# Token norms of a diffusion trunk: sums and modulated tiles formed in PSUM, mean squares from the token tiles, three filter units ahead of the first norm

## The chip, the cores and the metric

The kernel runs on one core of one Trainium2 chip. The metric is the device time of one execution in microseconds (us); each figure is the median of the runs named with it. TensorE is written PE in the profile's rows, VectorE DVE, ScalarE ACT, GpSimd POOL, SyncE SP.

## The reference

A trunk of four layers works on 256 latent tokens and 256 context tokens of 1,024 features (two "streams"). Each layer has a token mixer (layer 0 Hyena, 1 gated linear attention or GLA, 2 latent attention or MLA, 3 Hyena) and an MLP with squared ReLU. Each of these sub-layers first normalises and modulates its input:

```python
def rmsnorm(x, g):
    xf = x.astype(F32)
    y = xf * lax.rsqrt(jnp.mean(xf * xf, axis=-1, keepdims=True) + NORM_EPS)
    return (y * g.astype(F32)).astype(x.dtype)

def modulate(h, shift, scale):
    return h * (1 + scale) + shift

h_lat = modulate(rmsnorm(x_lat, norm1_g[i]), mod_l[0], mod_l[1])
x_lat = x_lat + mod_l[2] * y_lat
```

Shift, scale and gate are columns of `silu(c) @ ada_w[i] + ada_b[i]`, a vector of 6 x 1,024 per layer and stream (the "maps", in six parts of 1,024). Hyena convolves with long filters: a small network of position gives `h`, `h @ f_w4` gives the taps of two filters in both directions for each feature, which are decayed, divided by their absolute sum and transformed to spectra. After MLA only the latent stream goes on. The output is the latent stream after a last norm.

## The kernel before

**Layout.** The stream x lies transposed: eight tiles `x0` to `x7` of 128 features by 512 tokens (256 latent, 256 context). At the start eight token tiles `xr` (128 tokens by 512 features, L250) are loaded and TensorE transposes them into x (L325 to 329), VectorE copying from PSUM (L329).

**Products.** A product of fp32 values is made as three matmuls of rounded halves (L369 wh x uH, L370 wh x uL, L371 wl x uH). A slab of weights comes by DMA on SP's queue as `wraw` (5 buffers), ACT rounds it to `wh` (L359, 4 buffers), POOL subtracts to `wl` (L360, 4 buffers). On the activations' side ACT writes the high half `uH` and VectorE the low half `uL`.

**The norm of two streams** is `norm_mod` (L515), used five times: ahead of Hyena 0, its MLP, GLA, its MLP, and MLA. For each stream `token_rstd` (L481) squares eight x tiles (on ACT, L490; in the opening on POOL, L488), adds seven of them up on VectorE (L497), lets TensorE sum over features (L501) and forms 1/rms in `rsqrt` (L474 to 478: two steps on ACT, three on VectorE). `token_diag` (L510, VectorE) and one matmul (L524) spread it over a PSUM bank `rb`. Then for each of eight tiles k: VectorE multiplies x by scale and 1/rms into `t`, an SBUF tile named xr (L528), ACT adds the shift and rounds to uH (L529), VectorE makes uL (L530). The norm of one stream, `lone_norm` (L570 to 626), used in the rest, already holds its input and its running sum in PSUM (L584, L585, L592, L594); its statistics L599 to 615 use the same `rsqrt` and `token_diag` and lead to the matmul L610. The last norm of all calls `token_rstd` (L1642).

**The banks.** The eight PSUM banks are handed out by tags: mm two, cv three, ada one, st two. Buffers of one tag are handed out in the order in which the code asks for them. First products of Hyena's unit 0, of GLA and of MLA go to mm; of the MLP's first product, chunks 2 and 3 go to cv and the others to mm.

**The maps.** Each part of the maps takes eight slabs of 512 KB, multiplied as they come (L407 load, L410 matmul); `ada_part` (L388 to 394) writes the shifts and `adam`, the scales. `pump(n)` lets n slabs go into the program at the place where it is called.

**The opening.** After the filter network (L300, L309) comes the first norm, then `filters` (L896): eight units, each of `taps` (L813 to 848: load of w4r, ACT and POOL split it at L822 and L823, matmuls L832 and L833, decay, four POOL operations at L836 to L847), `scaled` (L850 to 868: column sums L854, L855, division and split) and `spectra` (L870 to 894: 24 matmuls of 256 columns, copies, a store). The units' temporaries have one buffer each. In the stretch that the profile calls unit 0 and 1, `project` makes the three parts of a 128-feature unit: unit 0 in halves of one stream each (144 matmuls of 256 columns), later ones over both streams (512 columns). Ahead of MLA the products of the latent stream (pq, 384 columns, to mm) and then the KV products (pk, 320 columns, mostly to cv) follow the norm.

**Order.** A planner places each engine's instructions in one static order; the order of the program is its priority. It chooses among what its own timeline holds ready. `tc.issue_after(x)` keeps what is in it behind x.

The norm's core, before:

```python
for k in range(KD):
    t = np_.tile([P, SEQ], F32, tag="xr", name=nm("xr"))
    sc, sh = a[:, which, k, r : r + 1], m[:, 3 * which, k, r : r + 1]
    nc.vector.scalar_tensor_tensor(t, xT[k][:, s], sc, rb[:, :SEQ], ALU.mult, ALU.mult)
    nc.scalar.activation(uH[k][:, s], t, AF.Identity, bias=sh)
    nc.vector.scalar_tensor_tensor(uL[k][:, s], t, sh, rounded(uH[k][:, s]), ALU.add, ALU.subtract)
```

Of the kernel before, what the change touches and what calls it, by code (L numbers as in the profile page):

```python
# [18 lines left out]
P = 128  # L19
# [108 lines left out]
def trunk_kernel(ctx: ExitStack, tc: tile.TileContext, ins: dict, table, zpos, out, layers=(0, 1, 2, 3)):  # L128
# [123 lines left out]

    if need_hy:
# [70 lines left out]
    xT = [cp.tile([P, TOK], F32, tag=f"x{k}", name=f"x{k}") for k in range(KD)]  # L324
    for k in range(KD):  # L325
        ps = bank("cv")
        for j in range(4):
            nc.tensor.transpose(ps[:, j * P : (j + 1) * P], xr[2 * j + k // 4][:, (k % 4) * P : (k % 4 + 1) * P], ident)
        nc.vector.tensor_copy(xT[k], ps)  # L329
# [140 lines left out]
    def rsqrt(v, n):  # L470

        y = np_.tile([P, n], F32, tag="rs_y", name=nm("rsy"))
        t = np_.tile([P, n], F32, tag="rs_t", name=nm("rst"))
        nc.scalar.activation(t, v, AF.Ln)  # L474
        nc.scalar.activation(y, t, AF.Exp, scale=-0.5)
        nc.vector.scalar_tensor_tensor(t, y, -0.5, y, ALU.mult, ALU.mult)
        nc.vector.tensor_tensor(t, t, v, ALU.mult)
        nc.vector.scalar_tensor_tensor(y, t, 1.5, y, ALU.add, ALU.mult)
        return y

    def token_rstd(r, on_pool=False):  # L481

        s = slice(r * SEQ, (r + 1) * SEQ)
        acc = np_.tile([P, SEQ], F32, tag="sacc", name=nm("sacc"), bufs=1)

        def square(dst, k):
            if on_pool:
                nc.gpsimd.tensor_tensor(dst, xT[k][:, s], xT[k][:, s], ALU.mult)  # L488
            else:
                nc.scalar.activation(dst, xT[k][:, s], AF.Square)  # L490

        square(acc, 0)
        for k in range(1, KD):
            sq = np_.tile([P, SEQ], F32, tag="sq", name=nm("sq"))
            square(sq, k)
            if k < KD - 1:
                nc.vector.tensor_tensor(acc, acc, sq, ALU.add)  # L497
        ps = bank("st")
        for j in range(2):
            for e, a in enumerate((acc, sq)):  # L500
                nc.tensor.matmul(ps[:, 2 * j : 2 * j + 2], a[:, j * P : (j + 1) * P], ones[:, 0:2],  # L501
                                 start=e == 0, stop=e == 1)
        v = np_.tile([P, 2], F32, tag="rs_v", name=nm("rsv"))
        nc.vector.tensor_scalar(v, ps[:, 0:4:2], 1.0 / D, EPS, ALU.mult, ALU.add)
        return rsqrt(v, 2)

    def token_diag(y):
        diag = np_.tile([P, 2, P], F32, tag="sq", name=nm("diag"))
        for j in range(2):
            nc.vector.tensor_scalar(diag[:, j], ident, y[:, j : j + 1], None, ALU.mult)  # L510
        return diag
# [3 lines left out]
    def norm_mod(i, which, nt, first=False):  # L515
# [3 lines left out]
        uL = [up.tile([P, TOK], F32R, tag=f"uL{k}", name=nm("uL")) for k in range(KD)]  # L519
        def stream(r):  # L520
            s = slice(r * SEQ, (r + 1) * SEQ)
            y = token_rstd(r, first)
            rb = bank("st")
            nc.tensor.matmul(rb[:, :SEQ], ones, token_diag(y), start=True, stop=True)  # L524
            for k in range(KD):
                t = np_.tile([P, SEQ], F32, tag="xr", name=nm("xr"))
                sc, sh = a[:, which, k, r : r + 1], m[:, 3 * which, k, r : r + 1]
                nc.vector.scalar_tensor_tensor(t, xT[k][:, s], sc, rb[:, :SEQ], ALU.mult, ALU.mult)  # L528
# [42 lines left out]
    def lone_norm(i, which, mp):  # L571
# [27 lines left out]
        def statistics():  # L599
            ps = bank("st")  # L600
            for j in range(2):
                for e, a in enumerate((acc, sq)):
                    nc.tensor.matmul(ps[:, 2 * j : 2 * j + 2], a[:, j * P : (j + 1) * P], ones[:, 0:2],
                                     start=e == 0, stop=e == 1)
            v = np_.tile([P, 2], F32, tag="rs_v", name=nm("rsv"))
            nc.vector.tensor_scalar(v, ps[:, 0:4:2], 1.0 / D, EPS, ALU.mult, ALU.add)
            diag = token_diag(rsqrt(v, 2))
# [72 lines left out]
    def mlp(i, nt, later=None, lone=()):  # L680
        single = nt == SEQ
        if not single:
            u = norm_mod(i, 1, nt)
# [226 lines left out]
    def hyena(i, j, nt, build):  # L910

        two = nt == TOK
        if two:
            u = norm_mod(i, 0, nt, build)
        if not build:
            pump(8, 8)
        nct = 1 if two else 2
        units = KD // nct
        with tc.tile_pool(name=nm("hy"), bufs=2, reuse_waits="tile") as mp:
# [62 lines left out]
            if build:  # L982
                with tc.tile_pool(name=nm("fs"), bufs=1) as fp:
                    tabs = dft_table(fp, "dftt", fp, "odd")
                    ftab = dft_table(mp, "dftf", fp, "odd")
                    gtab = dft_table(mp, "dftg", fp, "odd")
                    for _ in filters(j, fp, tabs, "cv", False):
# [167 lines left out]
    def gla(i, j):  # L1155
# [4 lines left out]
        u = norm_mod(i, 0, nt)  # L1160
# [213 lines left out]
    def mla(i, j):  # L1374
        nt = TOK
        QR, KVR = 384, 256
        u = norm_mod(i, 0, nt)
# [226 lines left out]

    with tc.issue_after(chain.ins) if chain is not None else ExitStack():
        pump(14 if len(layers) == DEPTH else 38)
# [35 lines left out]
    y = token_rstd(0)  # L1642
# [39 lines left out]
```

## Time and profile before

| | |
|---|---|
| median of 3 runs | 2199.26 us (2194.21 to 2200.56) |
| the profiled execution | 2200.74 us |
| its span | 2199.0 us |
| mean granted clock of TensorE | 0.97 |

The span goes from the first to the last instruction that the trace records. In a timeline a row is the start, the duration, engine, line, operation, output and inputs; behind it, in brackets, the idle time of the engine before it and what ended that. Two operations of one engine overlap a little in such rows, as it is pipelined: "x2" with 0.86 us is two operations one behind the other. The granted clock is a share of 2.4 GHz; 0.50 is the lower of two levels, 1.2 GHz.

### The profile page before, as it was taken

What the parts mean: (1) busy time and instruction counts of PE and PEld (TensorE: products, weight loads), DVE (VectorE), ACT (ScalarE), POOL (GpSimd) and SP (SyncE); (2) the same over time, 40 slices, a digit from 0 to 9 for tenths busy, and PEclk for the clock granted to TensorE, in tenths of its full rate; (3) what the DMA queues carried; (4) which work ended last, traced back from release to release, by engine and by line L of the source; (5) the groups of instructions that cost most, each with busy time, mean ns of one, the idle gap of its engine ahead of it and who ended that gap; (6) DMA issues with size and microseconds to landing.
All of it is one profiled execution on the core that took longest, in us unless ns stands there. A gap on an engine that the chain in (4) does not pass through costs nothing. (4 is left out here: it accounts for less than half of the span.)

```text
span 2199.0 us, 33332 instructions
## 1 busy us (share of the span) xinstructions
PE 2076.9 (94%) x12834; PEld 1767.8 (80%) x12834; DVE 1300.7 (59%) x2442; ACT 907.8 (41%) x1529; POOL 1088.2 (49%) x637
## 2 busy tenths in 40 slices
PE   6998999989999999999889999998999998898998
PEld 3766687677888888878678777788789998888998
DVE  7863888765333335554675987677673224895323
ACT  2642333343333334554442222235445546544544
POOL 5662454346545433333224444334346887455885
PEclk8998999989999999999999999999999999999999
DMA  9666635533333332222216788853235665443663
GB/s 313 192 213 203 222 100 178 193 99 118 103 99 107 108 92 71 81 58 67 58 49 220 220 278 266 265 185 96 65 91 169 186 189 159 144 135 108 191 182 116
DMA packets 322301, 329.12 MB, mean 150 GB/s; under 512 B 21276, under 2 KB 248673, under 8 KB 322143
## 3 DMA queue, kind: packets, MB, share of 16 engines
q1 hardware_dynamic: 321012, 326.05, 47.8%
q8 instruction: 101, 1.65, 0.3%
q10 hardware_dynamic: 587, 0.61, 0.1%
q14 instruction: 57, 0.47, 0.1%
q0 software_dynamic: 544, 0.34, 0.1%
HBM read 317.51 MB, written 9.44 MB: 149 GB/s over the span
## 5 line engine op out<-in xcount | busy, mean ns | idle before, releaser
L360 POOL TENSOR_TENSOR wl<-wraw,wh 128x1024 fp32r<-128x1024 f32 (+2 forms) x378 | 907.1, 2413 | 898.7 <-ACT wh L359 850.9
L359 ACT CAST wh<-wraw 128x1024 fp32r<-128x1024 f32 (+2 forms) x378 | 391.0, 1042 | 634.0 <-PE mm L370 238.5
L369 PE MATMUL mm<-uH,wh 128*128 128x512 f32 (+3 forms) x1272 | 449.4, 356 | 15.0 <-ACT uH L584 5.4
L370 PE MATMUL mm<-uL,wh 128*128 128x512 f32 (+3 forms) x1272 | 449.3, 354 | 8.5 <-DVE uL L530 5.8
L371 PE MATMUL mm<-uH,wl 128*128 128x512 f32 (+3 forms) x1272 | 444.7, 351 | 0.0
L369 PEld LDWEIGHTS mm<-uH,wh 128*128 128x128 f32 (+1 forms) x1272 | 245.0, 194 | 58.2 <-issue 8.7
L370 PEld LDWEIGHTS mm<-uL,wh 128*128 128x128 f32 (+1 forms) x1272 | 246.3, 194 | 44.4 <-DVE uL L530 9.6
L371 PEld LDWEIGHTS mm<-uH,wl 128*128 128x128 f32 (+1 forms) x1272 | 245.9, 193 | 32.5 <-issue 3.8
L369 PE MATMUL cv<-fH,wh 128*128 128x512 f32 (+1 forms) x576 | 209.7, 370 | 9.6 <-ACT fH L176 6.7
L370 PE MATMUL cv<-fL,wh 128*128 128x512 f32 (+1 forms) x576 | 210.7, 367 | 0.7 <-DVE fL L177 0.6
L371 PE MATMUL cv<-fH,wl 128*128 128x512 f32 (+1 forms) x576 | 208.9, 366 | 0.0
L663 DVE SCALAR_TENSOR_TENSOR x<-cv,mods,x 128x256 f32<-128x256 f32 x256 | 112.2, 477 | 83.2 <-PE cv L371 83.2
L370 PE MATMUL sum<-fL,wh 128*128 128x256 f32 x512 | 138.8, 278 | 0.0
L369 PE MATMUL sum<-fH,wh 128*128 128x256 f32 x512 | 137.2, 278 | 0.0
L371 PE MATMUL sum<-fH,wl 128*128 128x256 f32 x512 | 136.7, 278 | 0.0
L369 PEld LDWEIGHTS cv<-fH,wh 128*128 128x128 f32 x576 | 108.0, 189 | 31.9 <-ACT fH L176 8.4
L715 DVE SCALAR_TENSOR_TENSOR mm<-mm,r 128x512 f32<-128x512 f32 x60 | 41.7, 696 | 139.9 <-ACT r L714 139.7
L370 PEld LDWEIGHTS cv<-fL,wh 128*128 128x128 f32 x576 | 108.6, 189 | 19.0 <-DVE fL L177 1.1
L371 PEld LDWEIGHTS cv<-fH,wl 128*128 128x128 f32 x576 | 108.6, 189 | 17.8 <-issue 0.2
L369 PE MATMUL mm<-oH,wh 128*128 128x256 f32 (+1 forms) x256 | 92.0, 361 | 18.9 <-DVE x L663 14.2
L436 DVE SCALAR_TENSOR_TENSOR st<-lw,sT,st 128x512 f32<-128x512 f32 x144 | 101.4, 747 | 9.8 <-DMA lw<-in_ada_w_dram 9.8
L618 DVE COPY rbias<-st 128x1 f32<-128x1 f32 x32 | 5.1, 159 | 163.1 <-PE st L371 162.8
(526 smaller groups left out, 4513.8 us busy)
## 6 DMA issues: line engine op xcount, KB each, us to landing
wraw<-in_mlp_w_dram SPq DMA_DIRECT2D x256, 512.0 KB
adaw<-in_ada_w_dram SPq DMA_DIRECT2D x96, 512.0 KB
lw<-in_ada_w_dram SPq DMA_DIRECT2D x96, 512.0 KB
wraw<-in_hy_w_in_dram SPq DMA_DIRECT2D x48, 512.0 KB
wraw<-in_gla_w_in_dram SPq DMA_DIRECT2D x24, 512.0 KB
spec<-S SPq DMA_DIRECT2D x16, 512.0 KB
wraw<-in_hy_w_out_dram SPq DMA_DIRECT2D x16, 512.0 KB
S<-spec SPq DMA_DIRECT2D x32, 256.0 KB
```

The lines of the kernel that those rows point to most:

```text
L359: nc.scalar.copy(wh[r0:r1, :n], raw[r0:r1, :n])
L360: nc.gpsimd.tensor_tensor(wl[r0:r1, :n], raw[r0:r1, :n], rounded(wh[r0:r1, :n]), ALU.subtract)
L369: nc.tensor.matmul(ps, lh, rh, start=start, stop=False)
L370: nc.tensor.matmul(ps, lh, rl, start=False, stop=False)
L371: nc.tensor.matmul(ps, ll, rh, start=False, stop=stop)
L436: nc.vector.scalar_tensor_tensor(dst, wt[:, cols], sT[:, k, 0:1], run[b], ALU.mult, ALU.add)
L618: nc.vector.tensor_copy(bias, ps[:, SEQ : SEQ + 1])
L663: add = nc.vector.scalar_tensor_tensor(xT[dt][:, q], ps[:, q], mods[i][:, gi, dt, r : r + 1], xT[dt][:, q], ALU.mult, ALU.add)
L715: nc.vector.scalar_tensor_tensor(r, r, 0.0, pos, ALU.max, ALU.mult)
```

## The change

The first norm's mean squares are taken from the token tiles: ACT squares each with a sum along the features, and one `rsqrt` of four columns serves both streams. The copies of x alternate between VectorE and ACT. Three units of the filters are put into the program ahead of the first norm, with 8 and 6 slabs of the maps between them in place of the 14 that stood behind the filter network. In the norm of two streams the running sum, the steps of 1/rms and the tile t lie in PSUM: t takes half a bank, two k to a bank, of the tag given (mm, or cv ahead of the MLP). Sums, 1/rms and `rb` of a stream share one st bank. ACT instead of VectorE makes the diagonal. ACT computes the Exp of 1/rms a second time, into PSUM. The statistics of the one-stream norm and the last norm use the same new `rsqrt` and `token_diag`.

```diff
+    def transpose_in(k):
...
+        (nc.scalar.copy if k % 2 else nc.vector.tensor_copy)(xT[k], ps)
...
+    sums = cp.tile([P, 8], F32, tag="xsum", name="xsum")
+    junk = wp.tile([P, SLOT], F32, tag="wl", name="junk", bufs=4)
+    for b in range(8):
+        nc.scalar.activation(junk[:, :512], xr[b], AF.Square, accum_out=sums[:, b : b + 1])
+    means = cp.tile([P, 4], F32, tag="xmean", name="xmean")
+    nc.vector.tensor_tensor(means, sums[:, 0:8:2], sums[:, 1:8:2], ALU.add)
+    nc.vector.tensor_scalar(means, means, 1.0 / D, EPS, ALU.mult, ALU.add)
...
-    def rsqrt(v, n):
+    def rsqrt(v, n, ps=None):
...
         nc.scalar.activation(t, v, AF.Ln)
         nc.scalar.activation(y, t, AF.Exp, scale=-0.5)
-        nc.vector.scalar_tensor_tensor(t, y, -0.5, y, ALU.mult, ALU.mult)
+        y2 = y
+        if ps is not None:
+            y2 = ps[:, :n]
+            nc.scalar.activation(y2, t, AF.Exp, scale=-0.5)
+            t = ps[:, n : 2 * n]
+        nc.vector.scalar_tensor_tensor(t, y2, -0.5, y, ALU.mult, ALU.mult)
         nc.vector.tensor_tensor(t, t, v, ALU.mult)
         nc.vector.scalar_tensor_tensor(y, t, 1.5, y, ALU.add, ALU.mult)
...
-    def token_rstd(r, on_pool=False):
+    def token_rstd(r, ps):
...
+        run = ps[:, :SEQ]
         acc = np_.tile([P, SEQ], F32, tag="sacc", name=nm("sacc"), bufs=1)
...
+        for k in range(KD):
+            sq = np_.tile([P, SEQ], F32, tag="sq", name=nm("sq")) if k else None
+            nc.scalar.activation(sq if k else run, xT[k][:, s], AF.Square)
+            if 0 < k < KD - 1:
+                nc.vector.tensor_tensor(acc if k == KD - 2 else run, run, sq, ALU.add)
+        st = ps[:, SEQ : SEQ + 4]
...
+        return rsqrt(v, 2, ps[:, SEQ + 4 : SEQ + 8])
...
-            nc.vector.tensor_scalar(diag[:, j], ident, y[:, j : j + 1], None, ALU.mult)
+            nc.scalar.activation(diag[:, j], ident, AF.Copy, scale=y[:, j : j + 1])
...
-    def norm_mod(i, which, nt, first=False):
+    def norm_mod(i, which, nt, tag, known=None):
...
-            y = token_rstd(r, first)
-            rb = bank("st")
-            nc.tensor.matmul(rb[:, :SEQ], ones, token_diag(y), start=True, stop=True)
+            ps = bank("st")
+            y = token_rstd(r, ps) if known is None else known[:, 2 * r : 2 * r + 2]
+            rb = ps[:, :SEQ]
+            nc.tensor.matmul(rb, ones, token_diag(y), start=True, stop=True)
             for k in range(KD):
-                t = np_.tile([P, SEQ], F32, tag="xr", name=nm("xr"))
+                if k % 2 == 0:
+                    t2 = bank(tag)
+                t = t2[:, k % 2 * SEQ : (k % 2 + 1) * SEQ]
...
-        u = norm_mod(i, 0, nt, build)
         if not build:
+            if two:
+                u = norm_mod(i, 0, nt, "mm")
             pump(8, 8)
...
                     tabs = dft_table(fp, "dftt", fp, "odd")
+                    spectra_ = filters(j, fp, tabs, "cv", False)
+                    next(spectra_)
+                    pump(8)
+                    next(spectra_)
+                    pump(6)
+                    next(spectra_)
+                    u = norm_mod(i, 0, nt, "mm", rsqrt(means, 4))
                     ftab = dft_table(mp, "dftf", fp, "odd")
                     gtab = dft_table(mp, "dftg", fp, "odd")
-                    for _ in filters(j, fp, tabs, "cv", False):
+                    for _ in spectra_:
                         pump(1, 8)
...
     pump(2)
-
-    with tc.issue_after(chain.ins) if chain is not None else ExitStack():
-        pump(14 if len(layers) == DEPTH else 38)
```

The MLP calls `norm_mod` with tag cv, GLA and MLA with mm; `statistics` of the one-stream norm and the last norm pass their st bank to `rsqrt`.

## Rows read from the trace of the kernel before

**Rows 1.** The page's first part: busy time, share of the span, instructions per engine.

```profile
PE 2076.9 (94%) x12834; PEld 1767.8 (80%) x12834; DVE 1300.7 (59%) x2442; ACT 907.8 (41%) x1529; POOL 1088.2 (49%) x637
```

**Rows 2.** Windows, 41.0 to 85.2: length; PE, PEld, DVE, ACT, POOL busy; clock, DMA, GB/s.

```profile
41.00:85.20 44.20, 40.35 (x263) 30.77 (x264) 39.77 (x61) 24.05 (x42) 26.52 (x19) 0.81 0.83 253
```

**Rows 3.** Timeline of the opening; from 79.33 to 85.07 there are 49 matmuls.

```profile
40.49 0.47 DVE L528 SCALAR_TENSOR_TENSOR xr<-x,adam,st 128x256 f32<-128x256 f32 x1
...
55.32 0.58 PE L370 MATMUL mm<-uL,wh 128*128 128x256 f32 x1 [1.73 <-DVE uL L530]
...
79.33 0.38 PE L369 MATMUL mm<-uH,wh 128*128 128x256 f32 x1
...
85.19 0.40 PE L369 MATMUL mm<-uH,wh 128*128 128x512 f32 x1
```

**Rows 4.** Groups of PE, 41.0 to 85.2: busy us, mean ns | idle before.

```profile
L410 PE MATMUL ada<-adaw,sT 128*32 128x256 f32 x64 | 6.6, 465 | 0.0
L833 PE MATMUL cv<-w4l,h 64*128 64x512 f32 x4 | 2.3, 620 | 0.0
...
L832 PE MATMUL cv<-w4h,h 128*128 128x512 f32 x4 | 2.2, 590 | 0.0
L855 PE MATMUL cv<-ab,ones 128*1 128x256 f32 x4 | 1.2, 377 | 0.0
```

**Rows 5.** Groups of POOL, 41 to 180 us, all eight filter units.

```profile
L847 POOL TENSOR_TENSOR eo<-hd 128x512 f32<-128x512 f32 x8 | 11.8, 1476 | 0.2
L823 POOL TENSOR_TENSOR w4l<-w4r,w4h 64x512 fp32r<-64x512 f32 x8 | 11.6, 1453 | 3.8 <-ACT w4h L822 3.8
...
L842 POOL TENSOR_TENSOR ab<-ab,eo 128x512 f32<-128x512 f32 x8 | 10.3, 1285 | 1.0 <-ACT eo L841 1.0
```

**Rows 6.** Single lines, whole span: ns minimum/median/maximum, first and last start, forms.

```profile
L530 DVE SCALAR_TENSOR_TENSOR uL<-xr,mods,uH x80: 466/483/3628, 41.6 to 1524.3; 128x256 fp32r<-128x256 f32 x80
L497 DVE TENSOR_TENSOR sacc<-sacc,sq x66: 407/418/2315, 18.2 to 2190.2; 128x256 f32<-128x256 f32 x66
L585 DVE SCALAR_TENSOR_TENSOR uL<-sum,adam,uH x24: 472/476/485, 1645.3 to 1998.3; 128x256 fp32r<-128x256 f32 x24
L594 DVE TENSOR_TENSOR mm<-mm,sq x15: 417/433/433, 1648.5 to 1999.2; 128x256 f32<-128x256 f32 x15
L528 DVE SCALAR_TENSOR_TENSOR xr<-x,adam,st x80: 461/473/483, 40.5 to 1522.4; 128x256 f32<-128x256 f32 x80
```

**Rows 7.** L530 by norm: 0 to 100, 425 to 480, 820 to 880, 1480 to 1530 us.

```profile
L530 DVE SCALAR_TENSOR_TENSOR uL<-xr,mods,uH 128x256 fp32r<-128x256 f32 x16 | 13.0, 828 | 1.8 <-ACT uH L529 1.8
...
L530 DVE SCALAR_TENSOR_TENSOR uL<-xr,mods,uH 128x256 fp32r<-128x256 f32 x16 | 13.1, 839 | 0.4 <-ACT uH L529 0.4
...
L530 DVE SCALAR_TENSOR_TENSOR uL<-xr,mods,uH 128x256 fp32r<-128x256 f32 x16 | 9.4, 611 | 0.7 <-ACT uH L529 0.7
...
L530 DVE SCALAR_TENSOR_TENSOR uL<-xr,mods,uH 128x256 fp32r<-128x256 f32 x16 | 12.0, 781 | 1.4 <-ACT uH L529 1.3
```

**Rows 8.** Timeline of the norm ahead of MLA, DVE and PE.

```profile
1498.02 0.44 PE L369 MATMUL mm<-wh,uH 128*128 128x384 f32 x1
...
1509.17 2.09 DVE L478 SCALAR_TENSOR_TENSOR rsy<-rst,rsy 128x2 f32<-128x2 f32 x1
...
1516.33 0.33 PE L371 MATMUL mm<-wh,uL 128*128 128x384 f32 x1
...
1520.11 0.86 DVE L528 SCALAR_TENSOR_TENSOR xr<-x,adam,st 128x256 f32<-128x256 f32 x2
```

**Rows 9.** Windows, all engines, ahead of the first MLP's products (columns as in rows 2).

```profile
475.00:480.00 5.00, 3.28 (x8) 2.61 (x9) 5.00 (x8) 3.97 (x8) 5.00 (x2) 0.50 0.59 166
```

**Rows 10.** Timeline of the one-stream norm ahead of the last MLP.

```profile
2006.87 2.34 DVE L476 SCALAR_TENSOR_TENSOR rst<-rsy 128x2 f32<-128x2 f32 x1 [0.95 <-ACT rsy L475]
2009.63 2.57 DVE L510 TENSOR_SCALAR diag<-ident,rsy 128x128 f32<-128x128 f32 x2
...
2012.25 0.70 PE L610 MATMUL st<-diag,ones 128*128 128x256 f32 x2 [3.65 <-DVE diag L510]
```

More of the change, by code (lines that the diff above doesn't have):

```diff
@@ L251, in trunk_kernel @@
         xr.append(t)
+    def transpose_in(k):
+        ps = bank("cv")
+        for j in range(4):
+            nc.tensor.transpose(ps[:, j * P : (j + 1) * P], xr[2 * j + k // 4][:, (k % 4) * P : (k % 4 + 1) * P], ident)
+        (nc.scalar.copy if k % 2 else nc.vector.tensor_copy)(xT[k], ps)
     if need_hy:
@@ L324, in trunk_kernel @@
     xT = [cp.tile([P, TOK], F32, tag=f"x{k}", name=f"x{k}") for k in range(KD)]
+    sums = cp.tile([P, 8], F32, tag="xsum", name="xsum")
[5 more added lines that the diff above has]
+    nc.vector.tensor_scalar(means, means, 1.0 / D, EPS, ALU.mult, ALU.add)
     for k in range(KD):
[L326 to L329, printed above, removed]
+        transpose_in(k)
     pre = nc.scalar.preload_act_table_set("natural_log_exp_and_others")
@@ L479, in rsqrt @@
         return y
-    def token_rstd(r, on_pool=False):
+    def token_rstd(r, ps):
         s = slice(r * SEQ, (r + 1) * SEQ)
+        run = ps[:, :SEQ]
         acc = np_.tile([P, SEQ], F32, tag="sacc", name=nm("sacc"), bufs=1)
[L486 to L498, printed above, removed]
+        for k in range(KD):
[4 more added lines that the diff above has]
+        st = ps[:, SEQ : SEQ + 4]
         for j in range(2):
             for e, a in enumerate((acc, sq)):
-                nc.tensor.matmul(ps[:, 2 * j : 2 * j + 2], a[:, j * P : (j + 1) * P], ones[:, 0:2],
+                nc.tensor.matmul(st[:, 2 * j : 2 * j + 2], a[:, j * P : (j + 1) * P], ones[:, 0:2],
                                  start=e == 0, stop=e == 1)
         v = np_.tile([P, 2], F32, tag="rs_v", name=nm("rsv"))
-        nc.vector.tensor_scalar(v, ps[:, 0:4:2], 1.0 / D, EPS, ALU.mult, ALU.add)
-        return rsqrt(v, 2)
+        nc.vector.tensor_scalar(v, st[:, 0:4:2], 1.0 / D, EPS, ALU.mult, ALU.add)
+        return rsqrt(v, 2, ps[:, SEQ + 4 : SEQ + 8])
     def token_diag(y):
@@ L521, in stream @@
             s = slice(r * SEQ, (r + 1) * SEQ)
-            y = token_rstd(r, first)
-            rb = bank("st")
-            nc.tensor.matmul(rb[:, :SEQ], ones, token_diag(y), start=True, stop=True)
+            ps = bank("st")
+            y = token_rstd(r, ps) if known is None else known[:, 2 * r : 2 * r + 2]
+            rb = ps[:, :SEQ]
+            nc.tensor.matmul(rb, ones, token_diag(y), start=True, stop=True)
             for k in range(KD):
-                t = np_.tile([P, SEQ], F32, tag="xr", name=nm("xr"))
+                if k % 2 == 0:
+                    t2 = bank(tag)
+                t = t2[:, k % 2 * SEQ : (k % 2 + 1) * SEQ]
                 sc, sh = a[:, which, k, r : r + 1], m[:, 3 * which, k, r : r + 1]
-                nc.vector.scalar_tensor_tensor(t, xT[k][:, s], sc, rb[:, :SEQ], ALU.mult, ALU.mult)
+                nc.vector.scalar_tensor_tensor(t, xT[k][:, s], sc, rb, ALU.mult, ALU.mult)
                 nc.scalar.activation(uH[k][:, s], t, AF.Identity, bias=sh)
@@ L600, in statistics @@
             ps = bank("st")
+            st = ps[:, SEQ : SEQ + 4]
             for j in range(2):
                 for e, a in enumerate((acc, sq)):
-                    nc.tensor.matmul(ps[:, 2 * j : 2 * j + 2], a[:, j * P : (j + 1) * P], ones[:, 0:2],
+                    nc.tensor.matmul(st[:, 2 * j : 2 * j + 2], a[:, j * P : (j + 1) * P], ones[:, 0:2],
                                      start=e == 0, stop=e == 1)
             v = np_.tile([P, 2], F32, tag="rs_v", name=nm("rsv"))
-            nc.vector.tensor_scalar(v, ps[:, 0:4:2], 1.0 / D, EPS, ALU.mult, ALU.add)
-            diag = token_diag(rsqrt(v, 2))
+            nc.vector.tensor_scalar(v, st[:, 0:4:2], 1.0 / D, EPS, ALU.mult, ALU.add)
+            diag = token_diag(rsqrt(v, 2, ps[:, SEQ + 4 : SEQ + 8]))
             def rstd():
@@ L682, in mlp @@
         if not single:
-            u = norm_mod(i, 1, nt)
+            u = norm_mod(i, 1, nt, "cv")
         with ExitStack() as es:
@@ L912, in hyena @@
         two = nt == TOK
-        if two:
-            u = norm_mod(i, 0, nt, build)
         if not build:
+            if two:
+                u = norm_mod(i, 0, nt, "mm")
             pump(8, 8)
@@ L1159, in gla @@
         w_in = g["gla_w_in"][j]
-        u = norm_mod(i, 0, nt)
+        u = norm_mod(i, 0, nt, "mm")
         pump(8, 8)
@@ L1376, in mla @@
         QR, KVR = 384, 256
-        u = norm_mod(i, 0, nt)
+        u = norm_mod(i, 0, nt, "mm")
         pump(8, 8)
@@ L1641, in trunk_kernel @@
         transposed(k)
-    y = token_rstd(0)
+    y = token_rstd(0, bank("st"))
     transposed(KD - 1)
```

## The prediction

> **What bounds the kernel now.** I read the page's busy line first: TensorE is busy 2076.9 us of the 2199.0 us span [rows 1]. So about 122 us are all that can be won by better order, and an engine is worth speeding up only where TensorE stands still behind it. Next I cut the span by windows of TensorE. The first large loss is the stretch from the first modulated tile to the first product of Hyena's second unit, 41.0 to 85.2 us, where TensorE is busy for 40.35 us of 44.20 but at a granted clock of 0.81, and VectorE for 39.77 [rows 2]. The timeline of that stretch shows its frame: the first modulated tile begins at 40.49, the first 512-column product of unit 1 at 85.19, and in between TensorE waits for a low half on VectorE [rows 3]. The groups of TensorE [rows 4] say what it had to do there, those of POOL what a filter unit costs that engine [rows 5].
>
> Then I asked why VectorE is slow in the norms. The low half L530 takes 483 ns at its median and 3628 at its worst, the sum L497 418 and 2315; the same kinds of operation with one operand in PSUM never leave their price: L585 472 to 485, L594 417 to 433, and L528, which stands between the L530s in the same norms, 461 to 483 [rows 6]. An SBUF-only operation of VectorE is sometimes held for the length of a POOL subtraction; one that reads or writes PSUM is not. By norm, sixteen L530 should cost 16 x 0.483 = 7.7 us and cost 13.0 in the opening, 13.1 ahead of the first MLP, 9.4 ahead of GLA (ahead of the second MLP the same to 0.1) and 12.0 ahead of MLA: 5.3, 5.4, 1.7, 1.7 and 4.3 us are held time [rows 7]. 0.3% of this kernel, 6.6 us, is about what a measurement can tell from no change.
>
> **The opening.** Removed: POOL's 16 squares, 12 sums, four little products, both 1/rms chains. Added: 8 ACT squares, two small VectorE operations, one rsqrt of four columns; they need only the token tiles, there long before 40.49, when the first scales arrive, and the wait for these covers them, so I cost them at nothing; uncovered, eight squares of 512 columns would be between 8 x 0.42, the sum of 256 columns on VectorE [rows 6], and twice that: 3 to 7 us. Half of the x copies go to ACT, at nothing for the same reason.
>
> Moved: three filter units come ahead of the norm. Work that TensorE does in 41.0 to 85.2: unit 0's 144 products at (85.19 - 79.33)/49 = 0.12 us [rows 3] are 17.2; the ada slabs 6.6; two taps 2.2 + 2.3; two scale steps 1.2 for L855 and about as much for their column sums [rows 4]; one unit of spectra, 24 products x 0.12 = 2.9. Sum 33.6 of 44.2, so 10.6 are lost. Three units cost POOL 3 x (1.45 + 1.29 + 2 x 1.48) = 17.1 us [rows 5]; TensorE's part, 3 x (2.9 + 2.25 + 1.2) = 19.1 us, fits into what is now bare: the slabs' arrival and the norm. The norm starts later: the DFT table and one unit's taps and decay, 0.8 MB, stand ahead of slabs on SP's queue, 3 us at 253 GB/s [rows 2], up to 6 if all three units' do. Its 32 VectorE operations at about 0.43 (two L528 in 0.86 [rows 8]) take 13.9 us, with filter work between, so unit 0 starts at about 60 instead of the first products at 42; but from there it runs dense, and what stood behind it is done. I take 8 of the 10.6 back, the rest goes to the clock's second rise and gaps. Bounds: +14 (all of it and 3 idle us before 41) and -3 (the slabs 6 us late, 3 of it uncovered): **+8**.
>
> **Sums, 1/rms and t in PSUM; ACT makes the diagonal.** Per norm the held time can go. Ahead of the first MLP, VectorE and POOL are both busy all of 475 to 480 us while TensorE has 3.28 of 5 at half clock [rows 9]; of 5.4 I count 3, since the first products (four chunks per stream) end earlier but the two streams then leave a gap: **+3** (0 to +5.4). Ahead of GLA 1.7 held: **+1** (-3 to +5); ahead of the second MLP **0** (-5 to +2). In the single-stream norms two small operations were held, 2.34 us and 2.57 for two, with TensorE 3.65 us idle behind the last [rows 10]; the PSUM operand and ACT's diagonal take those away: **+4** (0 to +4.6). The final norm gains an Exp of two columns on the path of the end: **-0.3**.
>
> Here a rule speaks against the change. The rows have an L530-like operation with its source in PSUM at 476 ns against 483 from SBUF, a sum at 433 against 418 [rows 6]: the operand's place costs -7 to +15 ns. The Trainium skill, "VectorE: DVE Perf Modes", section on the TRN2 errata, lists 58 + FD cycles for SBUF to SBUF and 120 + FD for PSUM to SBUF, at 0.96 GHz, some 65 ns more for a PSUM source. By it 32 operations per norm cost 2 us more, and three such norms on the path take 6 off the sum. I go by the rows.
>
> **The banks.** This is the added wait. t takes a PSUM bank per two k, eight pairs per norm, out of two "mm" banks (three "cv" ahead of the MLP). The first products of Hyena, GLA and MLA also write "mm", and banks of a tag go round in turn, so none of them can begin before stream 1's sixth tile has left its bank. Behind the waiting product on TensorE stand the others of its chain; and the weight slabs that it holds keep the next ones out. In Hyena this costs nothing as long as filter work is there, which is why I start unit 0 at 60. Ahead of MLA there is no such work: now the 48 products of the latent stream begin at 1498.02, with stream 0's first halves, and end at 1516.33 [rows 8], while VectorE is still at stream 1. Stream 1's fifth and sixth tile are formed at 1520.11 and on. Of that, some 9 us are held time that goes: 4.3 in L530, 1.9 in one step of the 1/rms [rows 7, 8], and about 2.8 in the sums, an estimate within their worst single one, 2.3 against 0.4 [rows 6]. So the bank comes free near 1513, after the two L530 of that pair. The 48 products, of 384 columns each and so 1.5 x 0.12 = 0.18 us apart, are 8.6 us, and two more at half clock: an end at 1523.5, **-7** (0, where the KV products with "cv" banks go first; -10, where they wait for slabs too).
>
> **Sum.** 8 + 3 + 1 + 0 + 4 - 0.3 - 7 = 8.7 us gained against the profiled execution's own 2200.74, which stands 1.5 above the median of 2199.26: 2192.0, and 2190.5 against the median. I say **2190**.
>
> **Rivals.**
> 1. *The bank decides* (slower). For it: every first product of GLA, MLA and the MLPs' third and fourth chunk waits for a bank behind 32 VectorE operations, where now it starts on the first halves, and in such a stretch the granted clock was 0.50 [rows 9]. Against: before, the same products ran at DVE's pace anyway. Price: MLA 10, GLA 3, second MLP 5, the opening at its old pace and 3 late, less 4 from the single-stream norms and 3 at the first MLP: 14, so 2213. It decides once TensorE's idle time from a residual's end to the sixth tile exceeds the held time taken away (5.4 and 4.3 at the most).
> 2. *The opening does not do what it says*: TensorE has no slack later, and what is done early is only moved; the filters' pace is POOL's and ACT's. Then 0 in the opening, MLA -5, the rest as above: 2196.5.
> 3. *Opening recovered whole*, +14, MLA -3: 2180.
> 4. *PSUM operands are dear.* If each of VectorE's 32 operations per norm took 22 ns more, the spread of L528 in rows 6, on the path of three norms, 2 us would be lost: 2192.5. The medians of rows 6 speak against it. The Trainium skill's page on VectorE named above would have it at 6 us, 2196.5.
>
> **How the numbers follow.** Forecast 0.45, rival 1 0.19, rival 2 0.22, rival 3 0.12, rival 4 0.02. Faster by over 6.6 us is under 2192.7: 0.33 of the forecast, all of rival 3, 0.07 of rivals 2 and 4: 0.52. Within: 0.12 of the forecast, 0.16 of rivals 2 and 4: 0.28. Slower, over 2205.9: rival 1 and a remainder of rival 2, 0.20. The range goes from 2175, the opening at its bound with MLA unharmed, to 2210, two thirds of the way into rival 1. Both signs do not hold most of the chance alike: the forecast's own range is 2183 to 2198.
>
> **What would show it.** Right: L530 and L497 without long cases; in the opening three units of spectra before the first product of unit 0, which begins near 60 and runs at 0.12 us; unit 1's first 512-column product by 77 plus the moved filter work; MLA's first product at 1512 or so of the old time scale, with TensorE idle before it and at half clock after. Wrong: TensorE's windows between 41 and 100 with as much idle as before; GLA or the second MLP with a new wait of over 3 us on a t tile; L528 or L530 at 540 ns; or the held time still there, moved to another operation on SBUF alone (the squares' and filters' own).

## The result: slower, and where the profile after says so

The changed kernel takes 2221.35 us (median of 4 runs, 2219.48 to 2226.88), the kernel before 2197.04 in the same runs: a ratio of 1.0117, 95% interval 1.0099 to 1.0134. That is 24 us slower, outside the forecast's range and on its other side. The execution profiled after took 2226.88 (span 2225.1), the slowest of its four; that of before, 2200.74, was among the slower of its own too, and that of the last column below, 2170.40, the fastest of its six (median 2179.62). So stage times from the traces are good to some microseconds, and the medians carry the sums.

I cut the traces at the start of the last residual add of each stage, of the first add in the first row, and of the eighth (the last before a gap) in the row on MLA's first residual. Differences are after less before, in us; the other columns are experiments told below (1, 2 and 6), each against the same trace of before.

| to the end of | before | changed | preload held | copies only | norms alone |
|---|---|---|---|---|---|
| opening, layer 0's first add | 262.7 | -20.5 | -8.6 | +3.7 | -5.1 |
| layer 0's mixer | 436.3 | -5.5 | +1.0 | +12.3 | -7.8 |
| first MLP | 842.5 | -10.8 | -1.1 | +12.6 | -13.9 |
| GLA | 1119.3 | +11.3 | -6.6 | +36.0 | -16.8 |
| second MLP | 1500.4 | +8.9 | -8.0 | +38.9 | -20.5 |
| MLA's first residual | 1607.0 | +28.4 | +4.1 | +45.9 | -20.8 |
| last layer's MLP | 2188.9 | +22.9 | -1.3 | +46.7 | -32.0 |

Read downward, the changed kernel loses 15 in layer 0's mixer, 22 in GLA and 19.5 up to MLA's first residual, and wins in the MLPs and in the last layers. The page's first part after, which answers to [rows 1], shows TensorE with the same work and ScalarE 99 us busier (907.8 before):

```profile
PE 2078.6 (93%) x12818; PEld 1766.6 (79%) x12818; DVE 1238.8 (56%) x2397; ACT 1006.8 (45%) x1650; POOL 1074.9 (48%) x621
```

The part of the theory about held operations is right. Single lines after (ns minimum/median/maximum), which answer to [rows 6]: the low half is now L544, the modulated tile L542, the sum L506. Each has two forms, by the bank or tile that it reads or writes.

```profile
L544 DVE SCALAR_TENSOR_TENSOR uL<-mm,mods,uH x48: 462/476/486, 42.7 to 1527.6; 128x256 fp32r<-128x256 f32 x48
L544 DVE SCALAR_TENSOR_TENSOR uL<-cv,mods,uH x32: 465/477/485, 429.4 to 1151.5; 128x256 fp32r<-128x256 f32 x32
L542 DVE SCALAR_TENSOR_TENSOR mm<-x,adam,st x48: 467/484/491, 41.1 to 1526.5; 128x256 f32<-128x256 f32 x48
L542 DVE SCALAR_TENSOR_TENSOR cv<-x,adam,st x32: 477/484/490, 427.9 to 1150.5; 128x256 f32<-128x256 f32 x32
L506 DVE TENSOR_TENSOR st<-st,sq x45: 421/432/433, 407.3 to 2214.1; 128x256 f32<-128x256 f32 x45
L506 DVE TENSOR_TENSOR sacc<-st,sq x9: 386/415/424, 417.7 to 2214.7; 128x256 f32<-128x256 f32 x9
```

No case is longer than 491 ns, where L530 had gone to 3628 and L497 to 2315. By the medians of the larger groups, PSUM operands cost -7 ns in L544, +11 in L542, +14 in L506.

One of the prediction's own signs of being wrong came true: TensorE stands idle for longer between 41 and 100 us. Its windows (length; PE, PEld, DVE, ACT, POOL busy; clock, DMA share, GB/s), before and then after, leave 3.9 and 14.1 us idle:

```profile
41.00:100.00 59.00, 55.15 (x338) 42.57 (x339) 48.64 (x70) 35.59 (x64) 39.45 (x34) 0.86 0.75 224
```

```profile
41.00:100.00 59.00, 44.92 (x301) 33.59 (x301) 45.24 (x72) 29.93 (x50) 36.08 (x26) 0.80 0.82 233
```

ScalarE's extra time was in no step of the prediction. These are its groups of table loads, before and then after (busy us, mean ns | idle before):

```profile
L180 ACT ACT_TABLE_LOAD x1 | 1.3, 1283 | 0.7 <-PEq L1667 0.7
L331 ACT ACT_TABLE_LOAD x1 | 1.3, 1283 | 0.0
```

```profile
L485 ACT ACT_TABLE_LOAD x18 | 23.1, 1283 | 0.3
L484 ACT ACT_TABLE_LOAD x18 | 23.1, 1283 | 0.3
L1175 ACT ACT_TABLE_LOAD x13 | 16.7, 1283 | 0.2
L1242 ACT ACT_TABLE_LOAD x6 | 7.7, 1283 | 0.1
L1265 ACT ACT_TABLE_LOAD x4 | 5.1, 1283 | 0.1
L1174 ACT ACT_TABLE_LOAD x4 | 5.1, 1283 | 0.1
L301 ACT ACT_TABLE_LOAD x2 | 2.6, 1283 | 0.0
L180 ACT ACT_TABLE_LOAD x1 | 1.3, 1283 | 0.7 <-PEq L1687 0.7
L341 ACT ACT_TABLE_LOAD x1 | 1.3, 1283 | 0.0
```

67 loads of 1283 ns stand where two stood. L484 and L485 are Ln and Exp of the 1/rms, the lines from 1174 on GLA's gates. ScalarE's timeline of the opening after shows how it came about:

```profile
21.83 1.28 ACT L341 ACT_TABLE_LOAD   x1
...
24.17 0.20 ACT L484 ACTIVATE rst<-xmean 128x4 f32<-128x4 f32 x1
24.39 1.28 ACT L301 ACT_TABLE_LOAD   x1
25.68 0.42 ACT L301 ACTIVATE scr<-scr 128x256 f32<-128x256 f32 x1
26.12 1.28 ACT L485 ACT_TABLE_LOAD   x1
27.41 0.21 ACT L485 ACTIVATE rsy<-rst 128x4 f32<-128x4 f32 x1
...
29.60 1.28 ACT L301 ACT_TABLE_LOAD   x1
33.88 0.63 ACT L301 ACTIVATE scr<-scr 128x512 f32<-128x512 f32 x1 [2.99 <-DVE scr L300]
```

L341 is the kernel's preload of the one table that holds both Ln and Exp. The call behind it pins it to the ScalarE instruction traced just before. In the kernel before, that was a rounding of the filter network's result, so the preload stood behind the last sine. In the changed kernel it is the copy of the last x tile, which waits for no sine: the preload goes out at 21.83, two sines come after it and fetch their own table, and from then on nearly every Ln and Exp of the 1/rms fetches one (18 of 19 each), as does each change from one to the other in GLA's gates. TensorE waits behind this chain in a head of GLA (1.24 us at 929.60, for the `sg` of L1243; four such waits in GLA, 3.4 us, where run 1 below has none):

```profile
923.94 1.28 ACT L1175 ACT_TABLE_LOAD   x1
925.24 0.63 ACT L1175 ACTIVATE sg<-sg 128x512 f32<-128x512 f32 x1
...
926.89 1.28 ACT L1242 ACT_TABLE_LOAD   x1
...
929.35 1.28 ACT L1175 ACT_TABLE_LOAD   x1
...
931.30 1.28 ACT L1265 ACT_TABLE_LOAD   x1
```

The Trainium skill, "ScalarE: Activation LUTs", section "Table sets: the hidden batching unit", counts Ln followed by Exp as one load, because one set has both. The rows differ: L484 and L485 have a load each, 18 times over. One set served both only where the preload named it.

MLA's part looks otherwise. TensorE's timeline ahead of MLA's first products after, which answers to [rows 8]:

```profile
1511.43 0.36 PE L510 MATMUL st<-ones,sq 128*128 128x2 f32 x2
...
1517.79 1.22 PE L536 MATMUL st<-diag,ones 128*128 128x256 f32 x2 [6.00 <-ACT diag L519]
1526.16 0.69 PE L379 MATMUL mm<-wh,uH 128*128 128x384 f32 x1 [7.15 <-DVE uL L544]
```

The first product begins some 17 us behind the second MLP's last add (1509.3), where before it began 2.4 us ahead of it (1498.02 against 1500.4). It waits 7.15 us for VectorE's low halves although stream 0's were ready long since: the bank. The 6.00 us ahead hold two table loads. So two theories stood: **T**, the table loads, and **B**, the wait for a PSUM bank, which was the prediction's first rival.

### The profile page after: what moved, and what is told of

The parts are those of the page before. It is cut to its first block, busy times and chain, and to the rows that moved or that the text cites. A ratio compares the mean times of both kernels' runs of the same rounds, so it can differ in the third digit from the quotient of the medians.

```text
span 2225.1 us, 33349 instructions
## 1 busy us (share of the span) xinstructions
PE 2078.6 (93%) x12818; PEld 1766.6 (79%) x12818; DVE 1238.8 (56%) x2397; ACT 1006.8 (45%) x1650; POOL 1074.9 (48%) x621
## 5 line engine op out<-in xcount | busy, mean ns | idle before, releaser
L379 PE MATMUL mm<-uH,wh 128*128 128x512 f32 (+3 forms) x1272 | 444.2, 352 | 17.6 <-ACT uH L543 6.7
L379 PE MATMUL mm<-oH,wh 128*128 128x256 f32 (+1 forms) x256 | 94.1, 369 | 22.8 <-DVE x L678 16.8
L678 DVE SCALAR_TENSOR_TENSOR x<-mm,mods,x 128x256 f32<-128x256 f32 x176 | 79.4, 477 | 30.3 <-PE mm L381 29.5
```

The source lines that it names most:

```text
L379: nc.tensor.matmul(ps, lh, rh, start=start, stop=False)
L678: add = nc.vector.scalar_tensor_tensor(xT[dt][:, q], ps[:, q], mods[i][:, gi, dt, r : r + 1], xT[dt][:, q], ALU.mult, ALU.add)
```

## Experiments

All times are medians, in us; beside them stands the ratio to runs of the kernel before on the same chip, with its 95% interval. The ratio is worked out from all runs of both kernels and can differ a little from the quotient of the two medians. Runs 1 to 4, 5 to 8, 9 and 10, 11 and 12 stand on four chips, where the kernel before has medians of 2196.66, 2195.89, 2196.02 and 2194.79. The intervals reach 3 to 4 us either way, so a difference of under some 5 us between two of these runs is not clear of noise.

**1. The preload held behind the filter network.**

```diff
-            nc.scalar.copy(dst[:fw], hv[:fw])
+            h3_copy = nc.scalar.copy(dst[:fw], hv[:fw])
...
-    pre = nc.scalar.preload_act_table_set("natural_log_exp_and_others")
+    with tc.issue_after(h3_copy.ins):
+        pre = nc.scalar.preload_act_table_set("natural_log_exp_and_others")
```

> The changed kernel with one thing altered: the preload of ScalarE's function table (ln and exp together) is held behind the filter network's last copy, as it stood before the change, so that it comes after the last sine. Theory T (table loads): in the changed kernel the preload slipped ahead of two sines, since the last ScalarE instruction traced before it is now a copy of x; the sines fetch their own table back, and from there on each Ln and each Exp fetches one of its own: 67 loads of 1.28 us where there were 2. T expects 2 loads, the 22 us lost in GLA's mixer all but gone, some 5 to 8 of the 19.5 lost ahead of and in MLA's, and 3 to 5 elsewhere: 2185 to 2197 us against 2221 for the changed kernel. Theory B (the wait for a PSUM bank ahead of GLA's and MLA's first products makes the loss; table loads lie beside it): no more than 8 us back, 2213 or above.

2203.73 us, 1.0022 (1.0010 to 1.0034): two loads, and 18 us back. That is 7 above T's range, since with the preload held everything up to the first MLP's end comes 9.7 later than in the changed kernel; but GLA's part is T's throughout: it went from +22.0 against before to -5.6. The window from the first MLP's end to GLA's (length; PE, PEld, DVE, ACT, POOL busy; clock, DMA share, GB/s), in the changed kernel and here:

```profile
831.90:1130.80 298.90, 265.42 (x1448) 218.92 (x1447) 144.42 (x267) 178.70 (x303) 86.42 (x37) 0.94 0.21 61
```

```profile
841.60:1112.80 271.20, 254.08 (x1448) 213.58 (x1447) 146.21 (x267) 128.65 (x265) 88.17 (x37) 0.98 0.23 67
```

The same 1448 matmuls, 50 us less of ScalarE, 28 us less in length. What is left of the loss sits ahead of MLA: +12 in the table above.

**2. The copies alone in the kernel before.**

```diff
-        nc.vector.tensor_copy(xT[k], ps)
+        (nc.scalar.copy if k % 2 else nc.vector.tensor_copy)(xT[k], ps)
```

> The kernel before with one line of the change: four of the eight copies of x go to ScalarE; nothing else of the change, so no PSUM bank is asked for that was not before. The preload is then free to slip ahead of the sines. T expects some 69 table loads and a loss in every norm and in GLA: 2215 to 2235 us against 2197. B expects no change within 4 us, or a gain of 1 to 2 from VectorE's four copies fewer.

2247.54 us, 1.0222 (1.0209 to 1.0236), 51 us slower, above T's range: 69 loads, 23 us lost in GLA, 12 by the end of layer 0, 7 ahead of and in MLA. B expected nothing. One line in the opening, four copies of at most 0.59 us each in the changed kernel's timeline, makes the whole loss and more, and 1 takes the loads away with the copies in place. T is shown. By stage, GLA and MLA's part pay alike in both (23 and 7 us here, 28 and 7 between 1 and the changed kernel). But up to the first MLP's end this kernel is 13 later than before, while the changed kernel is 10 earlier than 1; part of that is what ScalarE may do early there (see 7).

**3. t in SBUF ahead of GLA and MLA**, on top of 1.

```diff
-                if k % 2 == 0:
+                if tag is None:
+                    t2 = np_.tile([P, SEQ], F32, tag="xr", name=nm("xr"))
+                elif k % 2 == 0:
                     t2 = bank(tag)
...
-        u = norm_mod(i, 0, nt, "mm")
+        u = norm_mod(i, 0, nt, None)
```

> As the first of these runs (preload held), and ahead of GLA and MLA the modulated tile t lies in SBUF again, one tile per k, so that GLA's and MLA's first products wait for no bank; sums, 1/rms and the diagonal stay as changed. If the bank is a second cause beside the tables: faster than the first run by 8 to 14 us, all of it between MLA's norm and its first products, GLA within 3. If the tables are the only one: within 3 us of the first run, or slower by up to 6, as the low halves are held behind GpSimd again (4.3 and 1.7 us before the change).

2195.25 us, 0.9988 (0.9974 to 1.0001): 8.5 faster than 1. From the second MLP's end to MLA's first residual it takes what it took before (-0.2), against +12.1 in 1; GLA's first part is 3 us longer than in 1. B is a second cause, in MLA.

**4. The opening alone in the kernel before**, with the preload held as in 1 and every norm's tiles in SBUF (the change's means, copies and three filter units ahead).

```diff
+    for b in range(8):
+        nc.scalar.activation(junk[:, :512], xr[b], AF.Square, accum_out=sums[:, b : b + 1])
...
+                    spectra_ = filters(j, fp, tabs, "cv", False)
+                    next(spectra_)
...
+                    u = norm_mod(i, 0, nt, rsqrt(means, 4))
...
-        pump(14 if len(layers) == DEPTH else 38)
```

> The kernel before with the opening alone: mean squares from the token tiles, copies of x alternating, preload held behind the filter network, three filter units ahead of the first norm, the first norm's 1/rms from the known means; every norm's sums, 1/rms and t stay in SBUF as before. If the opening's gain is real and kept: the first residual add of layer 0 comes some 20 us early, about 7 of it from slabs of the maps put off, and the time is 2184 to 2191 against 2197. If what the opening wins is handed back in the layer behind it: 2194 to 2199.

2208.39 us, 1.0047 (1.0033 to 1.0062). Not 2184 to 2191, and worse than handed back. The first residual add comes 7.8 us early; the end of layer 0's mixer is 3.4 late. More on this at 11.

**5. t in SBUF ahead of MLA alone**, on top of 1: the edit of 3, with its call changed in MLA only.

```diff
     def mla(i, j):
...
-        u = norm_mod(i, 0, nt, "mm")
+        u = norm_mod(i, 0, nt, None)
```

> The first of these runs (the changed kernel with the table preload held behind the filter network), and t in SBUF ahead of MLA alone; ahead of GLA it stays in PSUM. By stage, t in SBUF in both places was 12 us shorter from the second MLP's end to MLA's first residual and 3 us longer in GLA's first part. If the bank costs in MLA only: MLA's stage back to 107 us, GLA's as in the first run, and 2190 to 2194 us in all. If the bank's wait and the held low halves just trade places in both (the sum is set by something else): 2195 to 2200, as with SBUF in both.

2188.89 us, 0.9970 (0.9954 to 0.9986): 15 faster than 1, MLA's stage (from the second MLP's end to MLA's first residual) 106.9 against 118.7. The bank's cost lies ahead of MLA; the stage shows 12 of the 15.

**6. The norms alone**: the kernel before, with PSUM sums, 1/rms, t and ScalarE's diagonal in all norms but the opening's, and t in SBUF ahead of MLA; the opening untouched.

```diff
-            y = token_rstd(r, first)
+            y = first_rstd(r) if first else token_rstd(r, ps)
...
-            u = norm_mod(i, 0, nt, build)
+            u = norm_mod(i, 0, nt, None if build else "mm", build)
```

Here `first_rstd` is the old sum and 1/rms with squares on GpSimd.

> The kernel before with the norms alone: sums, 1/rms and t in PSUM, the diagonal on ScalarE, in all norms but the opening's, and t in SBUF ahead of MLA; the opening is that of before (squares on GpSimd, copies of x on VectorE, 14 slabs behind the filter network, no filter unit ahead). If the opening part is worth nothing or less, as its run alone (2208 against 2197) says: 2182 to 2190 us, at or under the kernel before by 7 to 14 us, from the first MLP (2 to 5), GLA (3 to 6), the second MLP (2) and the one-stream norms (4 to 5). If the opening's 6 us at the first residual add are needed for that: 2192 to 2198.

2179.62 us, 0.9931 (0.9913 to 0.9949): 16 us faster than before, the fastest version tried, and 2 below its range. So the opening part of the change, even with its preload held, takes 9 us of what the norms win (5 against 6).

**7. Only what is traced from the first norm on held behind the preload**, on top of 5.

```diff
-    ctx.enter_context(tc.issue_after(pre.ins))
...
                     next(spectra_)
+                    ctx.enter_context(tc.issue_after(pre.ins))
                     u = norm_mod(i, 0, nt, "mm", rsqrt(means, 4))
```

> As the run with t in SBUF ahead of MLA alone, but only what is traced from the first norm on is held behind the preload, so that ScalarE can round the filter's table and taps before the last sine, as it did in the changed kernel. If these early casts are what made the changed kernel's opening 10 us shorter than with the preload held (first residual add 242 against 254 us, 7 of the 12 from slabs put off): 4 to 8 us faster than that run. If the first taps stand behind the maps' slabs on TensorE anyway (they began at 40 us with the cast ready at 31): within 3 us of it.

2183.34 us, 0.9946 (0.9929 to 0.9963), 5.6 faster than 5, as the first theory had it, though only just clear of the intervals. It is the whole change but for t ahead of MLA, with both faults mended, 12.5 us under the kernel before.

**8. t ahead of MLA in the cv banks**, on top of 1.

```diff
     def mla(i, j):
...
-        u = norm_mod(i, 0, nt, "mm")
+        u = norm_mod(i, 0, nt, "cv")
```

> The first of these runs, with t ahead of MLA still in PSUM but in the three cv banks instead of the two mm banks: nothing but the tag of the bank. If what the first products of MLA wait for is the mm bank, the query products begin on stream 0's first halves again, as before the change, and the stage from the second MLP's end to MLA's first residual is 107 to 112 us instead of 119; in all 2192 to 2199. If PSUM residence itself delays them, or slabs do: 117 to 122 and 2201 to 2206. The key products, which go to cv, then wait in their place; they come later anyway.

2189.15 us, 0.9968 (0.9953 to 0.9983), below its range: the stage takes 108.5 against 118.7 in 1. The first 20 us of its norm and products by windows (columns as above), here:

```profile
1498.00:1508.00 10.00, 9.06 (x53) 8.18 (x52) 6.73 (x20) 7.21 (x18) 8.65 (x5) 1.00 0.61 168
1508.00:1518.00 10.00, 9.10 (x59) 8.43 (x58) 7.02 (x16) 5.14 (x13) 2.53 (x2) 1.00 0.47 131
```

And in run 1:

```profile
1492.00:1502.00 10.00, 2.44 (x10) 1.54 (x10) 8.50 (x24) 5.93 (x17) 3.50 (x2) 0.66 0.45 119
1502.00:1512.00 10.00, 5.46 (x17) 5.46 (x18) 5.36 (x12) 2.68 (x7) 0.00 (x0) 0.50 0.01 2
```

TensorE has 18.2 us of work against 7.9, at full clock against 0.66 and 0.50. Only the tag differs, t is in PSUM in both: it is the queue for the mm banks, not PSUM.

**9. The means without units ahead**, on top of 5: no filter unit before the first norm, the 14 slabs behind the network again, t of the first norm in SBUF.

```diff
-                    spectra_ = filters(j, fp, tabs, "cv", False)
-                    next(spectra_)
...
+            u = norm_mod(i, 0, nt, None, rsqrt(means, 4)) if build else norm_mod(i, 0, nt, "mm")
...
+        pump(14 if len(layers) == DEPTH else 38)
```

> As the run with t in SBUF ahead of MLA alone (2189), but the opening keeps only the means from the token tiles and the shared copies: no filter unit is put ahead of the first norm, the 14 slabs stand behind the filter network again, and t of the first norm lies in SBUF, so that unit 0's products start on the first halves. If the three units ahead are what makes the opening worth nothing: as fast as the norms alone (2180), 2176 to 2184. If the means and copies on ScalarE are what costs, or the preload held behind the filter network: 2186 to 2193.

2192.05 us, 0.9985 (0.9974 to 0.9996): by the second theory, 12 slower than 6. TensorE has been busy 1.3 us longer than in 6 by 160 us into the run, and 2.3 less by 200. The preload's hold can't be it by itself, since 6 has the same hold, behind the same copy. What is left are the means, the copies and the opening's diagonal on ScalarE; which of them loses was not taken further apart and stays open.

**10. The same with the preload's hold late**, as in 7.

```diff
-    ctx.enter_context(tc.issue_after(pre.ins))
...
+                with tc.issue_after(pre.ins):
+                    known = rsqrt(means, 4)
...
+                    ctx.enter_context(tc.issue_after(pre.ins))
                     for unit in range(2):
                         project(unit)
```

> As the other run of this pair, with ScalarE's work of the filters' first units free to go ahead of the table preload; the first norm's own Ln and Exp and all that follows the filters are held behind it. If early casts are worth what they were with three units ahead (2183 against 2189): 4 to 6 us faster than the other run. If they only count when a unit is ahead of the norm: within 2 us of it.

2190.26 us, 0.9984 (0.9970 to 0.9997): within 2 of 9, as the second theory had it: no gain from early casts shows without a unit ahead of the norm.

**11. The norms alone, and the opening's t in the mm banks.**

```diff
-            u = norm_mod(i, 0, nt, None if build else "mm", build)
+            u = norm_mod(i, 0, nt, "mm", build)
```

> The norms alone (2179.6), and the opening's norm too has its t in the two mm banks; its squares, sums and 1/rms stay as before. Between 40 and 65 us VectorE is busy for 9.4 to 9.8 of every 10 us and its low halves are held behind GpSimd. If that is what the opening loses: 4 to 8 us faster than the norms alone, the first residual add of layer 0 earlier by as much. If unit 0's products, which then wait for a bank until stream 1's sixth tile, lose what VectorE wins: 2178 to 2188, the first products at about 60 instead of 46.

2190.18 us, 0.9982 (0.9970 to 0.9994): 10.6 slower than 6, a little above the second theory's range. Unit 0's first product begins at about 70 instead of 46 us, and the first residual add still comes 4.2 earlier than in 6. The loss lies behind it, in layer 0's last part. There the maps' slabs show it. TensorE's group of slab products from 360 to 440 us (busy, mean ns | idle before), first in the kernel before:

```profile
L410 PE MATMUL ada<-adaw,sT 128*32 128x256 f32 x158 | 13.4, 388 | 2.9 <-DMA adaw<-in_ada_w_dram 2.9
```

The same group in the changed kernel, and then in 7:

```profile
L420 PE MATMUL ada<-adaw,sT 128*32 128x256 f32 x216 | 18.8, 418 | 6.8 <-DMA adaw<-in_ada_w_dram 6.8
```

```profile
L420 PE MATMUL ada<-adaw,sT 128*32 128x256 f32 x216 | 18.9, 414 | 7.7 <-DMA adaw<-in_ada_w_dram 7.6
```

And in 6, then in this run:

```profile
L411 PE MATMUL ada<-adaw,sT 128*32 128x256 f32 x158 | 13.4, 388 | 3.1 <-DMA adaw<-in_ada_w_dram 3.1
```

```profile
L411 PE MATMUL ada<-adaw,sT 128*32 128x256 f32 x176 | 16.5, 420 | 8.0 <-DMA adaw<-in_ada_w_dram 8.0
```

By the first residual add the kernel before and 6 have taken 62.5 of the 96 slabs, this run 60, runs 1, 4 and 5 59, the changed kernel and 7 only 52. (The loop over filter units pumps one slab a unit; the three units drawn ahead of it pump none of these, which is three of them.) From the third residual's end to the fourth's, 12 slabs are left in the kernel before and in 6, 14 in 1, 4, 5 and here, 20 in the changed kernel and 7, and TensorE waits for their DMA. That stretch takes 49.0 us here, 11 more than in 6, about the whole loss. In 6 it takes 37.9 us at a clock of 1.00 (window, columns as above):

```profile
390.80:428.70 37.90, 34.54 (x282) 26.88 (x282) 25.36 (x51) 12.92 (x28) 10.86 (x7) 1.00 0.57 195
```

In 7 it takes 52.0 at 0.90, with TensorE busy for 9.8 us more:

```profile
380.60:432.60 52.00, 44.36 (x350) 31.45 (x353) 27.92 (x55) 14.37 (x31) 9.94 (x8) 0.90 0.63 212
```

That the slabs put off make this loss is argued from the traces: no run moved the slabs alone. And it is not the loss of 9 and 10: there 64 slabs are taken by the first add, 9 are left, and the same stretch takes 36 us.

**12. The squares thrown into PSUM**, on top of 7.

```diff
-    junk = wp.tile([P, SLOT], F32, tag="wl", name="junk", bufs=4)
+    junk = bank("st")
```

> The run with the whole change, the preload held only from the first norm on and t in SBUF ahead of MLA (2183), with one thing altered: the squares of the token tiles are thrown into a PSUM bank instead of one of the four wl slots, which the first slabs of the maps use as well. If the slot taken is why the opening wins nothing (slabs late): the first scales some 2 us earlier and 2 to 6 us less in all. If the slabs come at the pace of DMA (about 390 GB/s from 20 to 40 us with or without): within 3 us of 2183.

2184.54 us, 0.9945 (0.9928 to 0.9961), 1.2 from 7 and within its 3: the slot is not what the opening lacks.

## Why the prediction was wrong, by its own steps

- **"Half of the x copies go to ACT, at nothing for the same reason."** This is the step that failed, and it decided the sign. I asked what hides the copies' own time, not what is ordered by them. The preload was pinned to the last of them. Held in its old place (1), 18 us come back. With early casts kept as well, my estimate of the loads' cost is about 23: 7's 2183 with MLA's bank wait added (14.8, 1 against 5) would be 2198, and the changed kernel takes 2221. No rival held it.
- **The banks, -7, with -10 as the bound.** Right place and mechanism, too small: 12 us by the stage, 14.8 by the medians. In 1 the second MLP ends 8.0 earlier than before; on the time scale of before, its 48 products run from 1514.6 to 1525.8, where I had 1513 to 1523.5 and before they ended at 1516.7: 9 us. The rest are the 96 KV products. Before, some ran beside the norm's second half and the last ended at 1528.2; in 1 they all come behind the 48 and end at 1539.9. I had priced them only in the bound, and only by slabs. The rival that the bank decides at GLA too has not come: there the planner put first products that write cv and st ahead, and GLA won 5.6 with its t in PSUM (stage in 1), where I had 1.
- **The opening, +8.** Here the sign was wrong as well. The first add came 20 early in the changed kernel, 10.5 slabs of it (at most 6.7 us, by the 0.64 of a slab's row in the timeline) only moved; and the slabs then waited for DMA in layer 0's last part. By the end of that mixer nothing (5: +0.9) or little (7: -4.0) is left. In whole runs the opening costs 12 by itself (4) and 9 beside the new norms (5 against 6); 7's loss of 4 against 6 is within the intervals. That TensorE's part "fits into what is now bare: the slabs' arrival and the norm" was wrong too: in 1 the first spectra began at 59 us, against 69.7 before, since the first taps began only at 41, behind the last slabs of the first maps, though ScalarE and GpSimd had their halves ready at 33. So one unit's spectra, not three, stood ahead of unit 0's first product, which began at 72 (67 in 1), not 60. (Before it began at 46, not at 42 as the prediction reads it.) The second rival, with nothing for the opening, came nearest.
- **Sums, 1/rms and t in PSUM.** Right, and under-sized in sum: in 1 the first MLP's part wins 2 (3 forecast), GLA 5.6 (1), the second MLP's 1.4 (0). For the one-stream norms (4) the traces give no size: from MLA's last add to the last MLP's, 1 is 5.4 us shorter than before, but the runs with the same code there lie between 11 us shorter (6) and 1.4 longer (9). In 6, with the opening untouched, the medians give 16 against the forecast's 8.
- **The final norm, -0.3.** From the last add to the end the changed kernel takes 13.3 us against 10.1. One table load, 1.3 us, is on that path (2217.04); the other (2215.04) ends before the mean that its Ln waits for. Without any loads the runs with the new statistics still take 11.7 to 12.5, while 4, which has the old ones, takes 10.1. So the new statistics cost about 2, and in 6 most of it lies in the sums: the Ln begins 4.7 us behind the last add, against 3.1 before.
- **PSUM operands.** The rows held: -7 to +14 ns. The Trainium skill's "VectorE: DVE Perf Modes" has 65 ns in the section on the TRN2 errata; this trace doesn't agree.

With the table loads left out, by the estimate above, the kernel would have taken about 2198, no change. The range (to 2210) would have held that, but in part by luck: the opening and the bank came out some 20 worse than forecast (-4 for +8 by 7 against 6, -14.8 for -7), the norms 8 better.

## What to carry to other kernels

Before an instruction is moved to another engine or traced earlier, look for what is pinned to its neighbours: a preload or a hold that means "behind the last one traced" changes its meaning with any new last one. After such an edit, count the table loads in the trace first. A gain that shows at the first milestone is no gain until the work put off is counted at the next one; and a PSUM bank tag shared by a norm's tiles and the products behind it can make those products wait for nearly the whole norm, as here ahead of MLA, where nothing else could go first.

## What the runs showed of the hardware

- A table load takes 1283 ns, every one of 67, and the operation behind it can begin 0.01 us after its end (L485: 26.12 + 1.28, then 27.41). Interleaved Ln and Exp cost one load each once the preload stood ahead of a sine (18 and 18), and none with the preload behind the last one.
- ScalarE's rounding from a PSUM tile takes 474 ns (L543, 80 cases) against 508 from SBUF before (L529): a gain of 34 ns that I had not counted.
- Ahead of MLA in run 1 TensorE was busy for 2.4 us of the 10 from 1492 and the granted clock was 0.66 on average; for the next 10 it was 0.50, the lower level. At the same place in run 8 it was busy for 9 of 10 and the clock was 1.00.
- The low half on VectorE, with its tiles all in SBUF, took up to 3628 ns (L530, median 483); with t in PSUM it never took over 486 (L544; 80 cases each).
